# Inverting the 64x64 triangular systems of an RWKV-7 layer: substitution on VectorE cut to 16x16 blocks, the rest as small products on TensorE

## The chip, the core and the metric

The kernel runs on one core of one Trainium2 chip. The metric is the device time of one execution in microseconds (us), as the median of several runs. PE is TensorE (with PEld its weight loads), DVE is VectorE, ACT is ScalarE, POOL is GpSimd, SP is SyncE; L971 is line 971 of the kernel.

## The reference, cut to what matters

The model has two layers over 512 positions of 1024 channels, all in 32-bit floats. Layer 0 mixes positions by a spatial gate, layer 1 by RWKV-7, and a gated feed-forward block with a short convolution follows each. Only RWKV-7 is touched. Its heart is a recurrence over 512 positions in each of 16 heads of 64 channels:

```python
def step(state, inp):
    r_t, w_t, k_t, v_t, a_t, b_t = inp
    sa = jnp.einsum('bhvk,bhk->bhv', state, a_t)
    state = (state * w_t[:, :, None, :]
             + sa[..., None] * b_t[:, :, None, :]
             + v_t[..., None] * k_t[:, :, None, :])
    y_t = jnp.einsum('bhvk,bhk->bhv', state, r_t)
    return state, y_t
```

Taken in chunks of 64 positions, the recurrence inside a chunk is a triangular system: with L the strictly triangular 64x64 matrix of the products of a and b in the chunk, the inverse of (1 - L) gives all of the chunk's `sa` at once. There are 16 heads times 8 chunks, so 128 such systems.

## The kernel before

The program runs the phases one after another: gate layer, feed-forward, RWKV-7, feed-forward, final norm. Inside RWKV-7 four pieces matter.

**Pairs** (`pairs`, `decay`, `operands`, `products`): for each of 8 pairs of heads, the operands of the recurrence are made, mostly on DVE and ACT, and multiplied on PE (L893, L908). The masked products (L897 on DVE) hold the systems; ACT copies them into `ti[g]` (L898), where g is 0 for the pairs 0 to 3 and 1 for the pairs 4 to 7. So `ti[0]` and `ti[1]` each hold 64 systems, two to a column of blocks (one in the upper 64 partitions, one in the lower).

**Inversion** (`invert(g)`): each system is cut into 32x32 blocks. The 128 diagonal blocks of one g lie in one tile, 32 of them for each quarter of the partitions, and DVE's 32x32 transposes (L962) turn them so that a block fills the elements of one partition. Then the inverse of all 128 blocks is made at once by forward substitution: for each column j of 0 to 30, DVE multiplies (L970) and adds (L971) over 128 partitions and (31-j)(j+1) elements. Two transposes bring the inverses back (L976 into `z`, L977 into `y`, its transposed form), ACT copies `y` into the diagonal blocks of `ti` (L981), and two rounds of 32x32 products on PE, 64 in each (L991, L994), with copies by ACT between and behind (L999, L1001), make the off-diagonal block of each 64x64 inverse.

**Scan** (`scan(g)`): 8 chunks in order for each g. A chunk is a chain: PE products with the state (L1066, L1070), copy to `wt` by DVE (L1068), PE product with the inverse in `ti[g]` (L1079), copies to `vu` by DVE and ACT (L1080, L1081), PE products for the next state (L1086) and the output (L1091), and the sum into the next chunk's `vu` on DVE (L1089). In the chunk 1 the gate's weights are loaded by DMA and rounded by ACT and DVE (`gate_weights`). `finish` normalises two chunks at a time.

**Filling work**: the large 128x512 products of the key and value projections (`projections`, recorded at L284 to L286), the two small products of each value column (`value`, L790 and L804), and later the output projection (`project`).

The order is written by `weave`: a main generator is stepped, and after each of its steps a fill generator advances by `rate` and a side generator by `side_rate`, both in steps marked by `yield`. `RATES` holds these numbers. During the pairs 4 to 6 and then 7 the side generator is `invert(0)`; during `scan(0)` it is `invert(1)`. Each engine runs its queue in order. `invert` has one yield after the transposes, one for each two columns of the substitution, one behind the transposes back, and one for each half of a round of products.

Of the kernel before, what the change touches and what calls it, by code (L numbers as in the profile page):

```python
# [11 lines left out]
F32 = mybir.dt.float32  # L12
F32R = mybir.dt.float32r
AF = mybir.ActivationFunctionType
ALU = mybir.AluOpType
# [4 lines left out]
P = 128  # L20
# [30 lines left out]
NG = 2 * 16 + 8  # L51


COFF = dict(ident=0, bones=128, center=256, masks=384, smask=512, causal=1024, blk2=1152, one=1154, id2=1155)
NCST = 1219


def constants():
    c = np.zeros((P, NCST), np.float32)
    i = np.arange(P)  # L60
    same = (i[:, None] // C) == (i[None, :] // C)
    c[:, 0:128] = np.eye(P)
    c[:, 128:256] = same
    c[:, 256:384] = np.eye(P) - same / C
    s, t = (i % C)[:, None], np.arange(C)[None, :]
    c[:, 384:448] = s < t
    c[:, 448:512] = s <= t
# [4 lines left out]
    c[:, 1155:1219] = (i % C)[:, None] == np.arange(C)[None, :]  # L72
    return c


# [68 lines left out]
class Emit:  # L144
# [558 lines left out]
    def rwkv_main(self, r, ctx, gain):  # L703
        nc, tc, A = self.nc, self.tc, self.A
        V, S, G = nc.vector, nc.scalar, nc.gpsimd
# [5 lines left out]
        ip = r.ip  # L711
# [230 lines left out]
        def invert(g):  # L942

            tg = ti[g].rearrange("p i c t -> p (i c) t")
            Q = [(slice(64 * hd + 32 * b, 64 * hd + 32 * b + 32), slice(32 * b, 32 * b + 32))
                 for hd in range(2) for b in range(2)]

            def blocks(tag):  # L950
                return ip.tile([P, 32, 32], F32, tag=tag, bufs=1, name=self.uid(tag))

            x, li, tt = blocks("ix"), blocks("li"), blocks("tt")
            pr = ip.tile([P, 272], F32, tag="pr", bufs=1, name=self.uid("pr"))
            G.memset(tt, 0.0)
            G.memset(tt.rearrange("p s t -> p (s t)")[:, 0:1024:33], 1.0)
            for n, (rows, cols) in enumerate(Q):
                if g == 1 and n % 2 == 0:
                    V.tensor_copy(x[rows], tg[rows, :, cols])
                else:  # L960
                    S.copy(x[rows], tg[rows, :, cols])
            V.transpose(li.rearrange("p s t -> p t s"), x.rearrange("p u t -> p t u"))  # L962
            for _ in range(WAIT):
                yield
            for j in range(31):
                ni, nj = 31 - j, j + 1
                a = li[:, j, j + 1:32].unsqueeze(1).to_broadcast([P, nj, ni])
                b = tt[:, 0:nj, j].unsqueeze(2).to_broadcast([P, nj, ni])
                q = pr[:, 0:ni * nj].rearrange("p (c i) -> p c i", i=ni)
                V.tensor_tensor(q, a, b, ALU.mult)  # L970
                V.tensor_tensor(tt[:, 0:nj, j + 1:32], tt[:, 0:nj, j + 1:32], q, ALU.add)  # L971
                if j % 2 == 1:
                    yield

            z, y = blocks("ix"), blocks("li")
            V.transpose(z.rearrange("p u t -> p t u"), tt)  # L976
            V.transpose(y.rearrange("p u t -> p t u"), tt.rearrange("p s t -> p t s"))  # L977
            yield
            off = blocks("tt")
            for rows, cols in Q:  # L980
                S.copy(tg[rows, :, cols], y[rows])  # L981
            for i in range(2):
                for hf in range(2):
                    ps = self.acc("aux").rearrange("p (u t) -> p u t", t=32)
                    us = slice(16 * hf, 16 * hf + 16)
                    for u in range(16):
                        for hd in range(2):
                            b0, b1 = Q[2 * hd][0], Q[2 * hd + 1][0]
                            n = 16 * hf + u
                            if i == 0:  # L990
                                nc.tensor.matmul(ps[b1, u, :], tg[b0, n, 32:64], z[b0, n, :], start=True, stop=True,  # L991
                                                 tile_position=(b0.start, b1.start))
                            else:
                                nc.tensor.matmul(ps[b0, u, :], off[b1, n, :], y[b1, n, :], start=True, stop=True,  # L994
                                                 tile_position=(b1.start, b0.start))
                    for hd in range(2):
                        b0, b1 = Q[2 * hd][0], Q[2 * hd + 1][0]
                        if i == 0:
                            S.copy(off[b1, us], ps[b1])  # L999
# [283 lines left out]
```

## Time and profile before

| what | value |
|---|---|
| median of 3 runs (lowest, highest) | 1319.26 us (1318.08, 1319.82) |
| the profiled execution | 1317.32 us |
| its span, first to last instruction | 1315.5 us |
| PE, PEld, DVE, ACT, POOL busy, share of the span | 97%, 78%, 64%, 47%, 11% |
| mean granted TensorE clock | 0.978 |
| PE share of the chain that ended last | 78% |
| DVE share of that chain | 9% |

A PE that counts as busy need not be at its peak: matmuls overlap, and the end of each is modelled. The weight loads (PEld) have ends of their own, so their busy share tells better how tightly PE's work is packed. A group row reads: line, engine, operation, output and inputs, shapes, count, then busy time in us and mean ns of one, then idle time of the engine before it and what ended it. A 32-bit product leaves two records on PE, so the 128 products of L991 in the program (64 for each g) are 256 records. A row of windows has, behind the stretch and its length, the busy us of PE, PEld, DVE, ACT and POOL with the number of instructions, the granted TensorE clock, the share of the DMA engines and GB/s. A row of the chain of waits is a start, a length, and who held the chain.

### The profile page before, as it was taken

Reading aid. Unit: us, or ns where it says so; the run is one execution under the profiler, and the core shown is the slowest. Engines: PE = TensorE matmul, PEld = TensorE weight load, DVE = VectorE, ACT = ScalarE, POOL = GpSimd, SP = SyncE. Lnnn points to the kernel's source line nnn. Section 1 sums busy time; section 2 is a strip of 40 time slices with the busy share of each in tenths; the row PEclk is TensorE's granted clock in tenths of the full one; section 3 lists DMA queues with packets and bytes.
Section 4 is the critical chain, followed back from the end, with each engine's and each line's share of the span. In section 5 each row is a group of like instructions: output and inputs, shape, how many; then the busy total and the mean of one; then the engine's idle time right before and its main releaser. Section 6 shows DMA issues by size and latency. Waiting matters only on the chain.

```text
span 1315.5 us, 19526 instructions
## 1 busy us (share of the span) xinstructions
PE 1272.7 (97%) x7618; PEld 1031.3 (78%) x7618; DVE 848.5 (64%) x1365; ACT 623.8 (47%) x1062; POOL 142.8 (11%) x152
## 2 busy tenths in 40 slices
PE   8999999999999999999999998898999999999996
PEld 6878888888888888787777766676888888888886
DVE  5565488788874444865869785656687777772223
ACT  5444455555554333565657644333554444442221
POOL 3100200000000010310111012332300000000001
PEclk9999999999999999999979996999999999999998
DMA  7332345555556753245877786881333232333322
GB/s 259 88 113 80 106 151 170 167 168 174 166 173 211 224 150 108 79 136 157 251 220 205 225 209 147 207 221 41 96 96 97 96 96 96 97 92 91 101 89 76
DMA packets 100461, 188.55 MB, mean 143 GB/s; under 512 B 16912, under 2 KB 47760, under 8 KB 100368
## 3 DMA queue, kind: packets, MB, share of 16 engines
q10 hardware_dynamic: 36448, 109.46, 27.2%
q1 hardware_dynamic: 63920, 77.84, 20.7%
q8 instruction: 60, 0.98, 0.3%
q14 instruction: 33, 0.27, 0.1%
HBM read 146.70 MB, written 40.57 MB: 142 GB/s over the span
## 4 chain that ended last, share of the span: by engine, by line
PE 78%; DVE 9%; ACT 3%; issue 2%; DMA 2%; POOL 1%; ACTq 0%; DVEq 0%; SPq 0%; POOLq 0%
PE mm L284 8%; PE mm L285 8%; PE mm L286 8%; PE e L284 5%; PE e L286 5%; PE e L285 5%; PE us L284 5%; PE us L286 5%; PE us L285 5%; PE aux L284 5%; PE aux L286 5%; PE aux L285 5%; DVE tt L971 1%; DVE pr L970 1%; PE us L1066 1%
## 5 line engine op out<-in xcount | busy, mean ns | idle before, releaser
L212 ACT CAST wh<-w 128x512 fp32r<-128x512 f32 (+1 forms) x361 | 220.1, 612 | 398.8 <-PE mm L285 97.1
L213 DVE TENSOR_TENSOR wl<-w,wh 128x512 fp32r<-128x512 f32 x353 | 243.8, 692 | 186.9 <-ACT wh L212 182.8
L284 PE MATMUL mm<-mxh,wh 128*128 128x512 f32 x392 | 161.2, 412 | 0.6 <-DVE h L1166 0.4
L285 PE MATMUL mm<-mxl,wh 128*128 128x512 f32 x392 | 155.7, 397 | 0.6 <-DVE mxl L1139 0.6
L286 PE MATMUL mm<-mxh,wl 128*128 128x512 f32 x392 | 155.9, 398 | 0.3 <-DVE wl L213 0.3
L311 POOL TENSOR_TENSOR ss<-ss,sq 128x512 f32<-128x512 f32 x30 | 40.7, 1357 | 777.3 <-issue 594.8
L284 PEld LDWEIGHTS mm<-mxh,wh 128*128 128x128 f32 x392 | 74.8, 191 | 20.1 <-issue 3.2
L507 ACT ACTIVATE cv<-z,par 128x512 f32<-128x512 f32 x88 | 71.7, 817 | 36.0 <-DVE z L505 35.9
L286 PEld LDWEIGHTS mm<-mxh,wl 128*128 128x128 f32 x392 | 74.7, 191 | 17.3 <-DVE wl L213 0.6
L285 PEld LDWEIGHTS mm<-mxl,wh 128*128 128x128 f32 x392 | 74.8, 191 | 16.3 <-DVE mxl L1139 1.3
L284 PE MATMUL e<-mxh,wh 128*128 128x512 f32 x216 | 84.5, 391 | 0.0
L284 PE MATMUL us<-mxh,wh 128*128 128x512 f32 (+1 forms) x216 | 84.4, 391 | 0.0
L286 PE MATMUL us<-mxh,wl 128*128 128x512 f32 (+1 forms) x216 | 84.1, 389 | 0.0
L285 PE MATMUL us<-mxl,wh 128*128 128x512 f32 (+1 forms) x216 | 84.1, 389 | 0.0
L285 PE MATMUL e<-mxl,wh 128*128 128x512 f32 x216 | 84.0, 389 | 0.0
L286 PE MATMUL e<-mxh,wl 128*128 128x512 f32 x216 | 84.0, 389 | 0.0
L508 DVE SCALAR_TENSOR_TENSOR cv<-z,par,cv 128x512 f32<-128x512 f32 x88 | 66.1, 752 | 23.9 <-ACT cv L507 23.9
L284 PE MATMUL aux<-mxh,wh 128*128 128x512 f32 x208 | 81.2, 391 | 0.2 <-ACT wh L212 0.2
L286 PE MATMUL aux<-mxh,wl 128*128 128x512 f32 x208 | 81.1, 390 | 0.0
L285 PE MATMUL aux<-mxl,wh 128*128 128x512 f32 x208 | 80.9, 389 | 0.0
L509 DVE SCALAR_TENSOR_TENSOR cv<-z,par,cv 128x512 f32<-128x512 f32 x88 | 66.0, 752 | 2.9
L284 PEld LDWEIGHTS e<-mxh,wh 128*128 128x128 f32 x216 | 40.6, 188 | 8.7 <-issue 0.5
(1071 smaller groups left out, 2679.4 us busy)
## 6 DMA issues: line engine op xcount, KB each, us to landing
w<-in_wup ACTq DMA_DIRECT2D x88, 512.0 KB, 3.5
w<-in_wdn ACTq DMA_DIRECT2D x32, 512.0 KB, 3.6
st<-std SPq DMA_DIRECT2D x32, 384.0 KB, 5.8
std<-lq SPq DMA_DIRECT2D x32, 256.0 KB, 4.6
w<-in_wdn ACTq DMA_DIRECT2D x16, 384.0 KB, 3.3
w<-in_wsu ACTq DMA_DIRECT2D x8, 512.0 KB, 3.5
w<-in_wso ACTq DMA_DIRECT2D x8, 512.0 KB, 3.5
pw<-in_wk SPq DMA_DIRECT2D x16, 256.0 KB, 3.9
```

The source lines that it names most:

```text
L212: nc.scalar.copy(hi[r, :n], src)
L213: (lo_eng or nc.vector).tensor_tensor(lo[r, :n], src, hi[r, :n].bitcast(F32), ALU.subtract)
L284: mm(acc, wh, xh, start=first, stop=False)
L285: mm(acc, wh, xl, start=False, stop=False)
L286: mm(acc, wl, xh, start=False, stop=last)
L311: nc.gpsimd.tensor_tensor(self.ss, self.ss, self.sq, ALU.add)
L507: nc.scalar.activation(c, z[:, 2:], AF.Identity, scale=cw(2, i), bias=self.p("conv_b", l * 44 + i))
L508: nc.vector.scalar_tensor_tensor(c, z[:, 1:T + 1], cw(1, i), c, ALU.mult, ALU.add)
L509: nc.vector.scalar_tensor_tensor(c, z[:, 0:T], cw(0, i), c, ALU.mult, ALU.add)
L970: V.tensor_tensor(q, a, b, ALU.mult)
L971: V.tensor_tensor(tt[:, 0:nj, j + 1:32], tt[:, 0:nj, j + 1:32], q, ALU.add)
L1066: nc.tensor.matmul(us[H[hd], 0, i, :], ar(i, hd, 0), vu[:, hd, i, :], start=True, stop=True)
```

## The change

The substitution stops at 16x16 blocks. Each partition now inverts the two 16x16 diagonal blocks of its 32x32 block in one instruction (an access pattern whose second dimension steps from the one to the other), for the columns 0 to 14 instead of 0 to 30. The rest of each 32x32 inverse is put together by three stages of products, each with a 32x32 stationary operand and 16 moving columns, in the PSUM tag `aux`:

- stage one: 128 products for each g (32 in each quarter of the partitions) of the block in `ti` with `z`; before it, POOL sets the first 16 columns of the diagonal blocks in `ti` to zero (after the copies have read them). DVE adds an identity (new constant `id4`) while it moves the result to `w`.
- stage two: 64 products (only the first 32x32 block of each system) of `y` with `w`; ACT copies the result into `z`.
- stage three: 128 products of `w` with `y`; ACT copies the result into `y`.

Behind them the copies and the two rounds of 32x32 products stand as before. ACT also fills one half of `w` with the identity. `w` uses the buffer `tt`, which the two transposes back have to have read. The side rates are changed with the number of yields (21 before, 16 now).

```diff
-RATES = ((1.9, 2), (1.9, 6, 2.2), (0.8, 2, 2), (0.7, 2), (2, 2), (0.7, 6, 2.2))
+RATES = ((1.9, 2), (1.9, 6, 1.7), (0.8, 2, 1), (0.7, 2), (2, 2), (0.7, 6, 2))
...
+            for rows, cols in Q:
+                G.memset(tg[rows, :, cols.start:cols.start + 16], 0.0)
+            def diag(t, s0, t0, *ap):
+                return bass.AP(tensor=t.tensor, offset=32 * s0 + t0, ap=[[1024, P], [16 * 32 + 16, 2], *ap])
...
-            for j in range(31):
-                ni, nj = 31 - j, j + 1
...
+            for j in range(15):
+                ni, nj = 15 - j, j + 1
+                a = diag(li, j, j + 1, [0, nj], [1, ni])
+                b = diag(tt, 0, j, [32, nj], [0, ni])
+                o = diag(tt, 0, j + 1, [32, nj], [1, ni])
+                q = pr[:, 0:2 * ni * nj].rearrange("p (d c i) -> p d c i", d=2, i=ni)
                 V.tensor_tensor(q, a, b, ALU.mult)
-                V.tensor_tensor(tt[:, 0:nj, j + 1:32], tt[:, 0:nj, j + 1:32], q, ALU.add)
+                V.tensor_tensor(o, o, q, ALU.add)
...
+            def small(out, lhs, rhs, rows):
+                for n in range(32):
+                    for r0 in rows:
+                        nc.tensor.matmul(out[r0, n, :], lhs(r0, n), rhs(r0, n), start=True, stop=True,
+                                         tile_position=(r0.start, r0.start))
+            id4 = self.c("id4", 32).unsqueeze(1)
+            w = blocks("tt")
+            S.copy(w[:, :, 16:32], id4[:, :, 16:32].to_broadcast([P, 32, 16]))
...
+            q = bank()
+            small(q, lambda r0, n: tg[r0, n, col[r0.start]], lambda r0, n: z[r0, n, 0:16], quads)
+            V.tensor_tensor(w[:, :, 0:16], q, id4[:, :, 0:16].to_broadcast([P, 32, 16]), ALU.add)
+            yield
+            q = bank()
+            small(q, lambda r0, n: y[r0, n, :], lambda r0, n: w[r0, n, 0:16], firsts)
+            for r0 in firsts:
+                S.copy(z[r0, :, 0:16], q[r0])
+            yield
+            q = bank()
+            small(q, lambda r0, n: w[r0, n, :], lambda r0, n: y[r0, n, 16:32], quads)
+            S.copy(y[:, :, 16:32], q)
+            yield
```

New line numbers: L980 and L981 are the substitution (L970 and L971 before), L986 and L987 the transposes back, L993 all three stages, L1008 the sum into `w`, L1021 to L1041 the old copies and products (L981 to L1001), and from there on 40 more than before (L1066 is L1106).

**Where the instructions stand.** First place: PE's queue in `scan(0)`, from the chunk 2 to the chunk 4. `us_` and `e_` are the PSUM tiles of the scan's chunk products, `aux_` those of the inversion. Before, the chunk 2's last products are followed by both halves of the first round for g = 1:

```order
L1086 MATMUL us_7114<-vu_6976,cbt_6975 64x64 x8
L1091 MATMUL e_7115<-vu_6976,st_6974 64x64 x8
L991 MATMUL aux_7218<-ix_7175,ti_5021 32x32 x32
L991 MATMUL aux_7253<-ix_7175,ti_5021 32x32 x32
L1066 MATMUL us_7302<-vu_7107,st_7105 64x64
L1070 MATMUL e_7303<-vu_7107,st_7105 64x64
...
L1079 MATMUL us_7302<-wt_7312,ti_5020 64x64 x8
L1091 MATMUL e_7303<-vu_7107,st_7105 64x64
L1117 MATMUL aux_7325<-cst,y_6881 128x128 x4
L994 MATMUL aux_7334<-li_7176,tt_7213 32x32 x32
L994 MATMUL aux_7369<-li_7176,tt_7213 32x32 x32
L1086 MATMUL us_7302<-vu_7107,cbt_7106 64x64 x8
```

Now the three stages (L993) stand there, one piece between each two steps of the chunks 2 and 3, and the old rounds are spread over the chunks 3 and 4:

```order
L993 MATMUL aux_7488<-ix_7448,ti_5021 32x16 x128
L1106 MATMUL us_7632<-vu_7388,st_7386 64x64
...
L1157 MATMUL aux_7655<-cst,y_7186 128x128 x4
L993 MATMUL aux_7664<-tt_7486,li_7449 32x16 x64
L1119 MATMUL us_7632<-wt_7642,ti_5020 64x64 x8
L993 MATMUL aux_7741<-li_7449,tt_7486 32x16 x128
L1126 MATMUL us_7632<-vu_7388,cbt_7387 64x64 x8
L1131 MATMUL e_7633<-vu_7388,st_7386 64x64 x8
L1031 MATMUL aux_7896<-ix_7448,ti_5021 32x32 x32
L1106 MATMUL us_7940<-vu_7626,st_7624 64x64 x8
L1110 MATMUL e_7941<-vu_7626,st_7624 64x64 x8
L1031 MATMUL aux_7965<-ix_7448,ti_5021 32x32 x32
```

What moved: the first product of the inversion still stands behind the chunk 2's last one, but the inversion now ends in the chunk 4 instead of the chunk 3.

Second place: DVE's queue at the start of `scan(0)`. `rt` is the sum of a value column, `wt` and `vu` are the chunk 0's copies, `pr`, `tt`, `ix` and `li` belong to the inversion of g = 1. Before, the substitution is spread between the copies of the chunks 0 to 2:

```order
L806 TENSOR_TENSOR rt_4363<-mm_6863,v_6827 128x512
L970 TENSOR_TENSOR pr_6784<-li_6782,tt_6783 128x247
L971 TENSOR_TENSOR tt_6783<-tt_6783,pr_6784 128x13x19
L970 TENSOR_TENSOR pr_6784<-li_6782,tt_6783 128x252
L1068 COPY wt_6892<-us_6882 128x256
L971 TENSOR_TENSOR tt_6783<-tt_6783,pr_6784 128x14x18
L970 TENSOR_TENSOR pr_6784<-li_6782,tt_6783 128x255
L971 TENSOR_TENSOR tt_6783<-tt_6783,pr_6784 128x15x17
L1080 COPY vu_6773<-us_6882 64x256
```

Now all of it, and both transposes back, stand ahead of the chunk 0's first copy:

```order
L980 TENSOR_TENSOR pr_7085<-li_7083,tt_7084 128x30
L981 TENSOR_TENSOR tt_7084<-tt_7084,pr_7085 128x2x15
L807 TENSOR_TENSOR rt_4363<-mm_7168,v_7132 128x512
L986 STREAM_TRANSPOSE ix_7448<-tt_7084 128x32x32
L987 STREAM_TRANSPOSE li_7449<-tt_7084 128x32x32
L1108 COPY wt_7197<-us_7187 128x256
L1120 COPY vu_7074<-us_7187 64x256
```

What moved: the transposes back, which stood behind the chunk 2's copies, now stand directly ahead of the chunk 0's.

Third place: PE's queue in the pair 6 and 7, for g = 0. `mm_` tiles are the filling work, `us_` and `aux_` those of L893 (L894 now). Before, the first round of 32x32 products stands inside the pair 7's first products:

```order
L893 MATMUL us_6571<-ar_6353,bk_6358 128x128 x3
L991 MATMUL aux_6503<-ix_6494,ti_5020 32x32 x32
L893 MATMUL aux_6570<-ar_6353,bk_6358 128x128 x4
L893 MATMUL us_6571<-ar_6353,bk_6358 128x128
L804 MATMUL mm_6659<-rt_4362,wb_6657 128x512
L991 MATMUL aux_6587<-ix_6494,ti_5020 32x32 x32
```

Now the stages stand in the pair 6, with filling work between them:

```order
L993 MATMUL aux_6381<-ix_6323,ti_5020 32x16 x128
L285 MATMUL mm_6580<-mxh_5679,wh_6255 128x512
L286 MATMUL mm_6580<-mxl_5680,wh_6255 128x512
L287 MATMUL mm_6580<-mxh_5679,wl_6256 128x512
L285 MATMUL mm_6580<-mxh_5686,wh_6255 128x512
L993 MATMUL aux_6511<-tt_6379,li_6324 32x16 x64
```

What moved: the inversion's PE work starts about half a pair earlier than before, and its first round of 32x32 products now stands between the pairs 6 and 7.

More of the change, by code (lines that the diff above doesn't have):

```diff
@@ L51 @@
 NG = 2 * 16 + 8
-COFF = dict(ident=0, bones=128, center=256, masks=384, smask=512, causal=1024, blk2=1152, one=1154, id2=1155)
-NCST = 1219
+COFF = dict(ident=0, bones=128, center=256, masks=384, smask=512, causal=1024, blk2=1152, one=1154, id2=1155, id4=1219)
+NCST = 1251
 def constants():
@@ L72, in constants @@
     c[:, 1155:1219] = (i % C)[:, None] == np.arange(C)[None, :]
+    c[:, 1219:1251] = (i % 32)[:, None] == np.arange(32)[None, :]
     return c
@@ L953, in invert @@
             x, li, tt = blocks("ix"), blocks("li"), blocks("tt")
[L954 removed]
+            pr = ip.tile([P, 128], F32, tag="pr", bufs=1, name=self.uid("pr"))
             G.memset(tt, 0.0)
@@ L977, in invert, with bank @@
             V.transpose(y.rearrange("p u t -> p t u"), tt.rearrange("p s t -> p t s"))
+            yield
[7 more added lines that the diff above has]
+            S.copy(w[:, :, 16:32], id4[:, :, 16:32].to_broadcast([P, 32, 16]))
+            def bank():
+                return self.acc("aux").rearrange("p (u t) -> p u t", t=16)
+            col = {q[0].start: q[1] for q in Q}
+            quads, firsts = [q[0] for q in Q], [q[0] for q in Q[::2]]
+            q = bank()
[10 more added lines that the diff above has]
+            S.copy(y[:, :, 16:32], q)
             yield
```

3 lines of the change are left out of this document (removed).

## The prediction

> **What bounds the kernel now.** I read the page first (PE is busy for 97% of the span and carries 78% of the chain), then cut the part that the change touches into stretches: the pairs with the first inversion (700 to 757 us), the filling work before the scan (757 to 772), and `scan(0)` with the second inversion (772 to 839). Columns: PE, PEld, DVE, ACT, POOL busy, clock, DMA share, GB/s. The stretch 640 to 656 holds pairs without an inversion, 480 to 490 nothing but large products.
>
> ```profile
> 480.00:490.00 10.00, 10.00 (x45) 8.04 (x44) 3.33 (x5) 3.01 (x5) 0.00 (x0) 1.00 0.33 92
> ...
> 640.00:656.00 16.00, 15.80 (x139) 12.52 (x138) 13.72 (x21) 11.65 (x22) 2.69 (x3) 1.00 0.90 273
> ...
> 700.00:757.00 57.00, 54.14 (x621) 42.05 (x621) 47.78 (x105) 38.16 (x77) 5.93 (x4) 0.97 0.75 213
> 757.00:772.00 15.00, 14.34 (x78) 10.91 (x76) 11.43 (x26) 8.72 (x17) 2.92 (x6) 1.00 0.86 200
> ...
> 791.00:805.00 14.00, 9.11 (x221) 7.61 (x222) 11.61 (x25) 5.78 (x12) 3.33 (x4) 0.81 0.57 128
> 805.00:822.00 17.00, 15.83 (x292) 14.05 (x292) 5.21 (x14) 8.97 (x16) 2.63 (x3) 0.50 0.63 149
> ```
>
> Two engines are near their limit in the pairs: DVE with 47.78 of 57 us, and PE, whose weight loads fill 42.05 of 57 us (74%), against 78% without an inversion and 80% in pure large products. From 791 on it is different: a chain waits. The chain of waits shows both:
>
> ```profile
> 713.46 0.85 DVE tt L971
> 714.31 0.60 DVE lq L897
> ...
> 720.70 0.60 DVE dg L886
> ...
> 741.39 1.92 DVE ix L976
> 743.35 1.20 PE aux L991 x64
> ...
> 776.64 5.57 DMA w<-in_g
> ...
> 799.34 1.91 DVE ix L976
> 801.29 3.62 PE aux L991 x128
> ```
>
> In the pairs it runs over DVE's substitution and the pairs' own DVE work; in the scan it runs over the end of the substitution, a transpose and the first round of products. What these cost the scan is seen in where its chunks start (first row of the chunks 2 to 7, and of the next scan):
>
> ```profile
> 791.15 0.34 PE L1066 MATMUL us<-vu,st 128*64 128x64 f32 x4
> 804.85 0.49 PE L1066 MATMUL us<-vu,st 128*64 128x64 f32 x4
> 815.93 0.53 PE L1066 MATMUL us<-vu,st 128*64 128x64 f32 x4
> 822.13 0.53 PE L1066 MATMUL us<-vu,st 128*64 128x64 f32 x4
> 829.64 0.33 PE L1066 MATMUL us<-vu,st 128*64 128x64 f32 x2 [1.22 <-DVE vu L1089]
> 834.27 0.33 PE L1066 MATMUL us<-vu,st 128*64 128x64 f32 x2
> 839.19 0.34 PE L1066 MATMUL us<-vu,st 128*64 128x64 f32 x4
> ```
>
> The chunk 7 alone takes 839.19 - 834.27 = 4.9 us. The chunks 2 and 3, with the inversion's end among them, take 13.7 and 11.1.
>
> **The change part by part.** *DVE gives back.* The substitution's two lines, with three of their sizes:
>
> ```profile
> L970 DVE TENSOR_TENSOR pr<-li,tt 128x31 f32<-128x31 f32 (+15 forms) x62 | 22.2, 359 | 1.4
> L971 DVE TENSOR_TENSOR tt<-tt,pr 128x31 f32<-128x31 f32 (+15 forms) x62 | 23.0, 370 | 1.4
> ...
> L970 DVE TENSOR_TENSOR pr<-li,tt 128x60 f32<-128x60 f32 x4 | 0.8, 212 | 0.1
> L970 DVE TENSOR_TENSOR pr<-li,tt 128x135 f32<-128x135 f32 x4 | 1.2, 298 | 0.1
> L970 DVE TENSOR_TENSOR pr<-li,tt 128x256 f32<-128x256 f32 x2 | 0.8, 412 | 0.0
> ...
> L897 DVE TENSOR_TENSOR lq<-aux,cst 128x512 f32<-128x512 f32 x16 | 10.9, 682 | 9.7 <-PE aux L893 8.5 <-issue 1.1
> ```
>
> The 124 instructions took 45.2 us, 22.6 for each g. The 30 new ones of a g have 30 to 128 elements, 1360/15 = 91 on average; between the rows of 60 and 135 that is 212 + 86 x 31/75 = 248 ns, so 7.4 us. The sum into `w` reads 512 elements from PSUM, as L897 does: 0.7 us. DVE saves about 14.5 us for each g.
>
> *PE takes on.* 320 products for each g, 640 records (two each). The nearest rows are these, with the products of a whole array, of half rows and half columns, and of a quarter of each:
>
> ```profile
> 759.28 1.05 PE L790 MATMUL mm<-cst,v 128*128 128x128 f32 x8
> ...
> 795.93 0.68 PE L1091 MATMUL e<-vu,st 64*64 64x64 f32 x16
> ...
> 743.35 1.20 PE L991 MATMUL aux<-ix,ti 32*32 32x32 f32 x64 [1.66 <-DVE ix L976]
> 801.29 3.62 PE L991 MATMUL aux<-ix,ti 32*32 32x32 f32 x128 [4.68 <-DVE ix L976]
> ```
>
> 131, 42 and 19 ns a record. The two quarters of L991 run side by side, so the price follows the stationary columns over the tiles in use, about 1 ns for each column (128/1, 64/2, 32/2, plus a tail). The 16 moving columns should save nothing against 32. Stage two has two tiles: 128 x 19 ns = 2.4 us. Stages one and three use four tiles. If all four run side by side, each costs 256 x 9.5 = 2.4 us, so 7 us for each g; if no more than two do, 4.8 each, so 12 us. I take 7, since nothing in L991 shows two tiles in each other's way. At the clock of 0.50, by the row at 801.29 (28 ns), it is 11 to 18 us.
>
> A rule speaks against this. The Trainium skill, TensorE: Matmul & The Clock Gate, Part 1 (Wait — 56ns, not 53.3ns?), has a floor of about 25 ns from one matmul's start to the next, however small. By it 640 records would be an estimated 16 us for each g, and the change a clear loss. The 64 records in 1.20 us above, 19 ns each, lie below that floor, so the trace does not bear it out.
>
> *ACT and POOL.* ACT gains four copies for each g (two of 32x512 at 578 ns as L999, two of 128x512 at about 590 as L911), 2.3 us:
>
> ```profile
> L999 ACT COPY tt<-aux 32x512 f32<-32x512 f32 x8 | 4.6, 578 | 0.1
> ...
> 759.08 0.59 ACT L911 COPY bt<-us 128x512 f32<-128x512 f32 x1
> ```
>
> ACT has 19 us free in the pairs. POOL gains four memsets of 512 elements for each g, by the row below (1024 elements) at most 2.9 us; they wait for the copies of L961 and hold up the next POOL work behind them. POOL's 5.93 of 57 us hides that; without that cover the chunk 0's L1075 would be late by it.
>
> ```profile
> 756.05 1.43 POOL L955 MEMSET tt<- 128x1024 f32 x1 [27.68 <-PE aux L994]
> ```
>
> *Pairs, 700 to 757.* If DVE alone set the pace, 14.5 us would go. But PE's queue is the same plus 7 us. How tightly it can be packed, and what the clock took, these rows tell:
>
> ```profile
> 745.00:748.00 3.00, 3.00 (x10) 1.36 (x9) 1.44 (x3) 2.79 (x3) 0.00 (x0) 0.50 0.15 38
> ...
> 820.10:823.40 3.30, 3.30 (x53) 3.06 (x55) 2.26 (x5) 0.74 (x2) 2.72 (x3) 0.50 0.76 174
> ```
>
> Of the 42.05 us of loads, L991 and L994 have 256 records at 19 ns, 4.8 us; the other 37.3 us need 47.8 us at 78%, 40.1 at the 93% that narrow products reach (row at 820.10). With 4.8 + 7 that is 59.6 or 51.9, against 57 now. Most of the loads belong to large products (80%), so I take 84%: 44.4 + 11.8 = 56.2. The wait of 1.66 us ahead of L991 and the clock of 0.50 behind it are then gone. I forecast 1 us saved, between 6 saved and 5 lost (two tiles at a time, at 78% or a little better).
>
> *Start of the scan.* 757 to 772 is filling work that PE does at its own pace, and stays. But both transposes back (1.9 us each) now stand ahead of the chunk 0's `wt` copy, and ACT's fill of `w` waits for them with the chunk's `vu` copy and the gate's DMA queued behind. The chunks 0 to 2 start up to 3.8 us later; part of the transposes falls before the chunk's products end, so I take 1.3. The DMA of 5.57 us at 776.64 then holds the chunk 1 as before, so the DVE time freed there is worth nothing.
>
> *Chunks 2 to 5.* Two prices that are still missing:
>
> ```profile
> 769.90 1.10 PE L804 MATMUL mm<-rt,wb 128*128 128x512 f32 x2 [0.29 <-issue]
> ...
> L981 ACT COPY ti<-li 32x1024 f32<-32x1024 f32 x8 | 8.3, 1042 | 8.2 <-DMA wl<-wvd 4.2 <-DVE li L977 4.0
> ```
>
> The wait of 4.68 us before L991 goes, since the substitution ends before the chunk 0. Chunk 2: 4.9, the last L790 and L804 (1.05 + 1.10), stage one (2.4): 9.4 instead of 13.7. Chunk 3: 4.9 + 4.8 for the stages two and three + 1.2 for half of the first round, less 1.0 that falls into the chain's own gaps: 9.9 instead of 11.1. Chunk 4: 4.9 + 1.2 + 2.4 is 8.5, instead of 6.2; ACT's eight copies ahead of the `vu` copy (4 x 1.04 + 4 x 0.58 = 6.5) just fit. Chunk 5: about 7, from 7.5. Together 34.8 instead of 829.64 - 791.15 = 38.5. With the 1.3, the scan saves 2.5 to 3.
>
> Sum: 1 + 3 = 4 us from the profiled 1317.3, so 1313.3. That execution lies 1.9 under the median, which gives **1315.3 us** against 1319.26.
>
> **The rivals.** *Slower: the clock stays low in the chunks 3 to 5.* The granted clock fell to 0.50 with the idle time at 797, and these rows show what held it there:
>
> ```profile
> 809.80:813.20 3.40, 3.40 (x124) 3.24 (x124) 1.12 (x4) 1.39 (x3) 0.00 (x0) 0.50 0.41 97
> ...
> 823.00:839.00 16.00, 12.87 (x237) 10.79 (x235) 10.82 (x28) 4.62 (x12) 5.51 (x8) 0.99 0.89 201
> ```
>
> 3.4 us packed with nothing but L994's 32x32 products did not bring the clock back; the 3.3 us at 820.10, packed with 64-wide chunk products, did (0.99 behind it). So small products may count as idling, and the change adds 7 us of them where little else runs. Then the stages cost 11 instead of 7, the old rounds 7 instead of 4, the chunk products 2 more: 9 lost against the 4 saved above: +5, so 1324. It decides if more than one of the windows between the chunks 2 and 5 is granted 0.50. For it: the rows. Against it: the wait that dropped the clock is gone. The Trainium skill, TensorE: Matmul & The Clock Gate, Part 1, has the clock halved by an idle window of about 3.4 us and restored by a busy one; by that rule no drop would come, and the row at 809.80 differs from it.
>
> *Faster: DVE did set the pace in the pairs*, as the chain says. PE then packs better than 0.80, and the pairs give 6 and the scan 5: 1308. Against it: the 0.74 that PE has already.
>
> *No difference*: the stages cost on PE what DVE gives back, to within 2.6 us. For it: the count of the pairs above.
>
> **How the numbers follow.** About 0.2% (2.6 us) can be told from no change. The forecast's own case (2.6 to 8 us saved) has 0.38, the faster rival 0.14, no difference 0.23, slower 0.25: faster 0.52, same 0.23, slower 0.25. The range takes in the forecast, no difference, and most of both rivals: 1307 to 1324.
>
> **What would show it.** L980 and L981 together near 15 us; stage one near 2.4 us, not 4.8; no wait of PE over 1 us before the stage in the chunk 2; chunks 2 to 5 together near 35 us; the stretch from the first L962 transpose to the second inversion's copies unchanged within 5 us. The prediction is wrong if that stretch shrinks by 10, or if the clock reads 0.50 through the chunks 3 to 5.

## The result, and the profile after

The changed kernel takes 1352.12 us, the median of four runs (1350.52 to 1354.62); the kernel before took 1318.67 on the same chip. The ratio is 1.0258, with a 95% interval of 1.0235 to 1.0281: 33 us slower, where 4 us faster was forecast. The profiled execution has a span of 1348.7 us, against 1315.5. One execution of the run filler (2135 us) and one of cutonly (6496 us) fell far from all others and are left out of their medians below.

From the page of after, the busy time and the two queues that carry instructions:

```profile
PE 1294.1 (96%) x8898; PEld 1050.3 (78%) x8898; DVE 824.4 (61%) x1303; ACT 628.7 (47%) x1070; POOL 144.9 (11%) x160
...
q8 instruction: 70, 1.15, 0.3%
q14 instruction: 33, 0.27, 0.1%
```

and the row of q8 from the page of before:

```profile
q8 instruction: 60, 0.98, 0.3%
```

q8 brings PE's instructions, 16 KB in a packet. Ten packets more is what the change adds: 640 products, of two loads (PEld) and two passes (PE) each, are 2560 instructions, 256 to a packet. Neither the count of instructions nor this row was used in the prediction.

The groups by line of after, for the substitution and for the three stages (busy, mean ns | idle time before them and what ended it):

```profile
L980 DVE TENSOR_TENSOR pr<-li,tt 128x30 f32<-128x30 f32 (+7 forms) x30 | 7.9, 265 | 0.9
L993 PE MATMUL aux<-tt,li 32*32 32x16 f32 x256 | 7.7, 210 | 4.1 <-issue 4.1
L981 DVE TENSOR_TENSOR tt<-tt,pr 128x30 f32<-128x30 f32 (+7 forms) x30 | 7.5, 251 | 0.7
...
L993 PE MATMUL aux<-li,tt 32*32 32x16 f32 x512 | 6.6, 195 | 6.6 <-issue 6.6
...
L993 PE MATMUL aux<-ix,ti 32*32 32x16 f32 x512 | 5.2, 182 | 5.2 <-issue 5.2
```

DVE's part came out as forecast: 7.9 + 7.5 = 15.4 us for both g. The products have something new: idle time of 4.1 + 6.6 + 5.2 = 15.9 us that ended with "issue", so with no wait that the profile shows; one more hole, of 1.6 us, stands inside the chunk products behind them (L1126). Together they are 17.4 us. PE's timeline tells where it lies. The stages of the first inversion (start, length, and in brackets the idle time before):

```profile
726.63 2.01 PE L993 MATMUL aux<-ix,ti 32*32 32x16 f32 x218
731.84 0.73 PE L993 MATMUL aux<-ix,ti 32*32 32x16 f32 x38 [3.20 <-issue]
...
734.50 2.52 PE L993 MATMUL aux<-tt,li 32*32 32x16 f32 x86
738.56 1.35 PE L993 MATMUL aux<-tt,li 32*32 32x16 f32 x42 [1.54 <-issue]
...
746.23 1.69 PE L993 MATMUL aux<-li,tt 32*32 32x16 f32 x181
750.83 0.81 PE L993 MATMUL aux<-li,tt 32*32 32x16 f32 x75 [2.90 <-issue]
```

and of the second one, in the scan:

```profile
815.14 1.73 PE L993 MATMUL aux<-ix,ti 32*32 32x16 f32 x185
818.82 0.78 PE L993 MATMUL aux<-ix,ti 32*32 32x16 f32 x71 [1.96 <-issue]
...
825.62 3.07 PE L993 MATMUL aux<-tt,li 32*32 32x16 f32 x108 [2.55 <-issue]
...
831.81 1.90 PE L993 MATMUL aux<-li,tt 32*32 32x16 f32 x128 [1.86 <-issue]
835.54 1.89 PE L993 MATMUL aux<-li,tt 32*32 32x16 f32 x124 [1.82 <-issue]
```

No stage runs through. A run of products stops in the middle, with no operand that it would wait for, and goes on 1.5 to 3.2 us later. The piece between two holes at 831.81 has 128 passes and as many loads: exactly one packet. The packets' own records fit: one starts at 729.49 and takes 0.94 us, and PE goes on at 731.84; so it goes on 1.4 us behind the packet's end. The next two holes end 1.3 us behind a packet's end.

Where this leaves the chunks, from the first rows of the chunks 2 to 6 of after:

```profile
809.44 0.34 PE L1106 MATMUL us<-vu,st 128*64 128x64 f32 x4
819.58 0.30 PE L1106 MATMUL us<-vu,st 128*64 128x64 f32 x2
843.16 0.69 PE L1106 MATMUL us<-vu,st 128*64 128x64 f32 x8
854.81 0.69 PE L1106 MATMUL us<-vu,st 128*64 128x64 f32 x8
862.94 0.33 PE L1106 MATMUL us<-vu,st 128*64 128x64 f32 x2 [1.22 <-DVE vu L1129]
```

The chunks 2 to 5 take 862.94 - 809.44 = 53.5 us, against 38.5 before and 34.8 forecast; the chunk 3, with the stages two and three, takes 23.6. Two stretches of after, with the columns of the prediction's windows (the clock is the third from the end), add the clock:

```profile
820.00:840.00 20.00, 12.18 (x445) 11.03 (x442) 2.46 (x7) 3.15 (x5) 0.00 (x0) 0.50 0.50 115
840.00:855.00 15.00, 14.41 (x364) 13.27 (x362) 4.14 (x9) 9.13 (x16) 4.44 (x5) 0.50 0.40 94
```

In the first of them PE is idle for 7.8 of 20 us. The clock is 0.50 from 820.0 to 857.6, so also through the second, where PE is busy for 14.41 of 15 us.

The loss has two places of like size. From the first L970 (L980) to the scan's first product the time grows from 772.3 - 702.5 = 69.8 to 790.1 - 702.5 = 87.6 us, 17.8 more; `scan(0)` grows from 66.9 to 82.8, 15.9 more. The rest is as before.

### The profile page after: what moved, and what is told of

It is laid out like the page before. It is cut to its first block, busy times and chain, and to the rows that moved or that the text cites. A ratio compares the mean times of both kernels' runs of the same rounds, so it can differ in the third digit from the quotient of the medians.

```text
span 1348.7 us, 22052 instructions
## 1 busy us (share of the span) xinstructions
PE 1294.1 (96%) x8898; PEld 1050.3 (78%) x8898; DVE 824.4 (61%) x1303; ACT 628.7 (47%) x1070; POOL 144.9 (11%) x160
## 4 chain that ended last, share of the span: by engine, by line
PE 83%; DVE 4%; issue 3%; ACT 3%; DMA 2%; POOL 1%; ACTq 0%; DVEq 0%; SPq 0%; POOLq 0%
PE mm L285 8%; PE mm L286 8%; PE mm L287 8%; PE e L285 5%; PE e L287 5%; PE e L286 5%; PE us L285 5%; PE us L287 5%; PE us L286 5%; PE aux L285 5%; PE aux L287 5%; PE aux L286 5%; PE aux L993 1%; DMA w<-in_wo 1%; PE aux L909 1%
## 5 line engine op out<-in xcount | busy, mean ns | idle before, releaser
L287 PEld LDWEIGHTS mm<-mxh,wl 128*128 128x128 f32 x392 | 75.1, 192 | 17.6 <-DMA wl<-wkd 0.8
L509 DVE SCALAR_TENSOR_TENSOR cv<-z,par,cv 128x512 f32<-128x512 f32 x88 | 66.1, 752 | 23.9 <-ACT cv L508 23.9
```

What stands on the lines that cost most here:

```text
L287: mm(acc, wl, xh, start=False, stop=last)
L509: nc.vector.scalar_tensor_tensor(c, z[:, 1:T + 1], cw(1, i), c, ALU.mult, ALU.add)
```

## The experiments

Theory A, supply: PE takes short instructions faster than they can be brought, a packet of 256 in a fixed time, and the holes are PE waiting for the next packet. Theory B, clock: small products count as idling, the clock halves, and that costs the time. Theory C, price: a product on a 32x32 tile is far dearer than forecast.

**The products alone, behind the kernel's end ("tail").** On the kernel before:

```diff
+        def run(tiles, cols):
+            q = e.acc("aux")
+            for n in range(384):
+                r0 = 32 * (n % tiles)
+                r, o = slice(r0, r0 + 32), cols * (n % (T // cols))
+                mm(q[r, o:o + cols], ident[r, r], wide[r, o:o + cols], start=True, stop=True,
+                   tile_position=(r0, r0))
...
+        run(4, 16)
...
+        run(1, 16)
...
+        run(1, 128)
```

Expected: 

> The kernel before with a tail of TensorE work that nothing reads, behind the last phase: three runs of 384 products (1536 instructions, 6 packets of 256) with 32x32 stationary blocks: 16 moving columns on four tiles, 16 columns on one tile, 128 columns on one tile; eight products of 128x128 by 512 columns ahead of each and behind. Supply theory: the first two runs both take about 4 x 3.9 + 4 = 20 us in bursts of 256 records (loads and passes together) with a hole behind each, whatever the number of tiles; the third is slower than its packets (768 x 50 to 60 ns, about 42 us) and has no hole. Price theory: the run on four tiles has the holes, the run on one tile has none and takes 768 x 25 ns, 19 us, evenly. Clock theory: both run evenly, at 0.50 once the first 4 us have passed.

PE's timeline of the run on four tiles:

```profile
1310.92 2.06 PE L1283 MATMUL aux<-cst 32*32 32x16 f32 x220
1315.76 1.90 PE L1283 MATMUL aux<-cst 32*32 32x16 f32 x128 [2.77 <-issue]
1319.49 1.90 PE L1283 MATMUL aux<-cst 32*32 32x16 f32 x128 [1.83 <-issue]
1322.97 1.90 PE L1283 MATMUL aux<-cst 32*32 32x16 f32 x128 [1.58 <-issue]
1326.46 1.90 PE L1283 MATMUL aux<-cst 32*32 32x16 f32 x128 [1.58 <-issue]
1330.20 0.72 PE L1283 MATMUL aux<-cst 32*32 32x16 f32 x36 [1.84 <-issue]
```

and of the run on one tile with 16 columns:

```profile
1339.95 37.55 PE L1283 MATMUL aux<-cst 32*32 32x16 f32 x768
```

Nothing here waits for another engine, and from 1313.5 on the DMA is nearly idle. On four tiles, 128 passes and their loads go through in 1.90 us, then comes a hole; from one burst's start to the next it takes 3.5 to 3.7 us. The records of the five packets start at 1313.36, 1316.91, 1320.60, 1324.05 and 1327.60, the last four about 1.1 us behind the start of a burst, and PE goes on 2.4 to 2.6 us after a packet's start. That fits a next packet that is asked for only when the one before it is begun. So PE gets 256 instructions in about 3.6 us, 14 ns for each. On one tile an instruction takes 37.55 us / 1536 = 24 ns, and there is no hole at all. That is theory A with its number. The expectation of holes on one tile was wrong, since these products are slower than the supply; against C speaks that the dearer products, not the cheaper, run evenly. The third run, with 128 columns, was expected to take 42 us and took 158.5, so 206 ns a pass, nearly all of it at the clock of 0.50; the price of such products was forecast far too low.

The Trainium skill, Runtime: NRT & Kernel Launch, section Instruction fetch mechanics, has the instructions arrive in blocks of 16 KiB, 256 of them, the next one brought while the current one is executed; the runs agree. It calls that cost mostly hidden, since instructions are sent out slower than a block is filled. Here that does not hold: 1.90 us of work stand against 3.6 us of supply.

**What a pass costs ("prices").** Again a tail, of short runs that lie within the packets that are there:

```diff
+        for what in ((48, 32, 4, 16), (48, 32, 2, 16), (48, 32, 1, 16), (24, 64, 2, 64), (24, 64, 1, 64),
+                     (96, 32, 4, 256), (24, 32, 2, 256), (24, 64, 1, 256)):
+            large()
+            run(*what)
```

Expected: 

> The kernel before with a tail that nothing reads: short runs, each behind six products of 128x128 by 512 columns so that its packets are there: 48 products (192 instructions) of 32x32 by 16 columns on four tiles, on two, on one; 24 of 64x64 by 64 columns on two tiles and on one; then 96 of 32x32 by 256 columns on four tiles, 24 on two tiles, 24 of 64x64 by 256 columns on one. Supply theory: no hole in any run; a record (load or pass) costs about 5 to 6 ns on four tiles, 11 on two and 24 or less on one at full clock. Price theory: four tiles cost no less than two. Clock theory: the long run on four tiles counts as busy and keeps the full clock, that on two 32x32 tiles falls to 0.50; if even four tiles of 32x32 fall to 0.50, the products of the stages can hold the clock down by themselves.

PE's timeline: four, two and one tile with 16 columns, and the long run on four tiles.

```profile
1308.07 0.99 PE L1283 MATMUL aux<-cst 32*32 32x16 f32 x96
...
1314.34 1.69 PE L1283 MATMUL aux<-cst 32*32 32x16 f32 x96
...
1321.32 3.21 PE L1283 MATMUL aux<-cst 32*32 32x16 f32 x96
...
1344.98 10.56 PE L1283 MATMUL aux<-cst 32*32 32x256 f32 x192
```

No hole anywhere, at full clock. A pass with its load takes 10.3, 17.6 and 33.4 ns on four, two and one tile (10 to 12, 22 and up to 48 were expected). For a g that is 512 x 10.3 + 128 x 17.6 = 7.5 us: the forecast of 7 was right for the array's time, and C falls. The floor of about 25 ns from matmul to matmul (the Trainium skill, TensorE: Matmul & The Clock Gate, Part 1, Wait — 56ns, not 53.3ns?) is undercut on two and on four tiles. But in the supplied pace of the tail, 128 passes in 3.6 us, a pass takes 28 ns: for the long runs of this kernel, a count by that floor (an estimated 16 us a g) would have come near the truth, for another reason.

As for B: the 10.56 us on four tiles, with 256 columns, kept the full clock, whereas the one-tile run of the tail went on at 0.50, busy throughout:

```profile
1350.00:1370.00 20.00, 20.00 (x379) 20.00 (x378) 0.00 (x0) 0.00 (x0) 0.00 (x0) 0.50 0.01 2
```

So products on one small tile, without a hole, did not hold the full clock, and those on four tiles did. A long run of 16 columns on four tiles without holes was not made. The run on two 32x32 tiles, for which 0.50 was expected, kept 1.00, but lasted only 5.37 us.

**A quarter of the instructions ("quarter").**

```diff
-                for n in range(32):
+                for n in range(0, 32, 4):
...
-                        nc.tensor.matmul(out[r0, n, :], lhs(r0, n), rhs(r0, n), start=True, stop=True,
+                        nc.tensor.matmul(out[r0, n:n + 4, :], lhs(r0, n), rhs(r0, slice(n, n + 4)),
```

Expected: 

> Leaves out three of four products of every stage: each remaining one multiplies four systems' columns by the first system's block, so the values are wrong, while the same 512 columns move and every output column is written. 80 products a g instead of 320, so 320 instructions of TensorE (two loads and two passes each) instead of 1280. Supply theory (TensorE's instructions arrive in packets of 256, about 3.9 us apart when it outruns them): about 7 or 8 of the 10 added packets go (62 or 63 on the queue q8), the idle 'issue' time inside the products goes, and the time falls to 1312 to 1322. Clock theory (small products count as idling, the low clock costs the time): at most 10 of the 33 us come back, 1342 or more. Price theory (a product on a 32x32 tile costs far more than 9.5 ns a record): the time falls also, but what is left of the products still shows holes in proportion to their number.

Measured: 1328.91 us, ratio 1.0078 (1.0050 to 1.0107), 62 packets. Two thirds of the loss are gone with three quarters of the instructions, the 512 columns being the same, though the time lies 7 us over the expected range. Its stages run without such a hole, but holes come up behind them, in the old products and the scan's (PE's timeline):

```profile
810.13 0.75 PE L1031 MATMUL aux<-ix,ti 32*32 32x32 f32 x35
813.93 0.63 PE L1031 MATMUL aux<-ix,ti 32*32 32x32 f32 x29 [3.06 <-issue]
816.02 1.92 PE L1031 MATMUL aux<-ix,ti 32*32 32x32 f32 x64
...
821.86 1.11 PE L1119 MATMUL us<-wt,ti 64*64 64x64 f32 x14 [3.51 <-issue]
```

The two holes are about 256 instructions apart (127 passes and as many loads). The scan's own products are short too; the supply is used up by whatever stands in a row.

**Twice the products ("double").**

```diff
+                        for _ in range(2):
+                            nc.tensor.matmul(out[r0, n, :], lhs(r0, n), rhs(r0, n), start=True, stop=True,
+                                             tile_position=(r0.start, r0.start))
```

Expected: 

> Every product of the stages issued twice in a row, same result: 640 products and 2560 instructions a g, 80 packets. Supply theory: the ten further packets take 3.6 us each with next to nothing of it hidden, since the first ten have used up what lay ready: 36 us more, 1383 to 1395. Price theory without packets (8 us a g more at full clock, 16 at half): 1368 to 1380.

Measured: 1386.01 us, ratio 1.0508 (1.0482 to 1.0533), 80 packets. The first ten packets cost 33.4 us, the next ten 1386.0 - 1352.1 = 33.9: 3.4 us for each, both times, and in the pairs 17 us for five. The bound of C without packets (1380) is passed. The 3.4 us are the price of 256 such instructions here, not of a hole: the holes grew from 17.4 to 32.0 us, by 14.6 of the 33.9.

**Each half alone ("cutonly", "addonly").** The first leaves out the stages:

```diff
-            def small(out, lhs, rhs, rows):
...
-            small(q, lambda r0, n: w[r0, n, :], lambda r0, n: y[r0, n, 16:32], quads)
-            S.copy(y[:, :, 16:32], q)
-            yield
+            for _ in range(3):
+                yield
```

Expected: 

> The cut of the substitution alone: the three stages of products, the fill of w and their copies are left out, so the off-diagonal 16x16 parts are missing and the values are wrong; the three yields stay. It shows what the time given back by DVE (14.5 us a g) is worth. If PE sets the pace of the pairs, only its wait of 1.66 us and the 3.4 us at half clock go there, and in the scan the wait of 4.68 us with part of the low clock: 1308 to 1315. If DVE set the pace (the faster rival of the prediction), the pairs alone give 10 or more: 1296 to 1304.

The second adds products to the kernel before, and nothing else but the side rates for three more steps:

```diff
             yield
+            for lhs, rhs, rows in ((None, z, quads), (y, z, firsts), (z, y, quads)):
+                out = self.acc("aux").rearrange("p (u t) -> p u t", t=16)
+                for n in range(32):
+                    for r0 in rows:
+                        l = tg[r0, n, col[r0.start]] if lhs is None else lhs[r0, n, :]
+                        nc.tensor.matmul(out[r0, n, :], l, rhs[r0, n, 0:16], start=True, stop=True,
+                                         tile_position=(r0.start, r0.start))
+                yield
```

Expected: 

> The products alone: the substitution stays as before, and the same 320 products a g go into banks that nothing reads, between the transposes back and the first round (rates 2.5, 2.3, 2.5 for three more steps). Supply theory: 70 packets as in the changed kernel, the same holes, and nearly the whole loss: 1345 to 1360. If the loss comes from the new chain of copies and sums between the stages, or from POOL's memsets, most of it is gone: 1320 to 1330.

Measured: cutonly 1316.82 us, ratio 0.9992 (0.9980 to 1.0003), just over the expected 1308 to 1315; addonly 1351.84 us, ratio 1.0272 (1.0249 to 1.0296), 70 packets. The products alone give the whole loss, so nothing of it need be put down to copies, sums and memsets. And the time given back by DVE is worth, in this order of the work, at most 2.6 us by the interval. Another execution of the same kernel ("cutonly2"), of 1319.59 us, shows why:

Expected: 

> The cut of the substitution alone once more, for its trace (its first profiled execution took five times as long as all others and can't be read). 62 of TensorE's packets or fewer, no hole of 256 records. If PE sets the pace of the pairs, the scan starts within 4 us of 772 although DVE is busy some 14 us less there; what is gained at the first round of the scan (the wait of 4.68 us) is lost again at a later wait of the scan.

The stretch from the first L970 (L980) to the scan, in before and in cutonly2 (the fourth number is DVE's busy time):

```profile
702.50:772.30 69.80, 66.91 (x686) 51.65 (x685) 57.35 (x130) 44.45 (x87) 8.85 (x9) 0.98 0.79 215
```

```profile
700.50:770.90 70.40, 65.81 (x686) 51.14 (x685) 46.19 (x106) 44.41 (x87) 8.51 (x13) 0.98 0.79 213
```

and two rows of cutonly2's waits between 790 and 832 (waited for: us, times, longest; its L1079 is a chunk's first product, its L1007 the second round):

```profile
PE us L1079 <- DMA vu<-vtd: 4.0, 1, 4.0
...
PE aux L1007 <- issue: 2.0, 1, 2.0
```

In the pairs DVE is busy for 46.19 us instead of 57.35, and the stretch is no shorter: DVE did not set the pace there. Nor did PE pack tighter, being idle for 4.6 us instead of 2.9. In the scan the chunk 2 takes 6.4 us instead of 13.7, as the vanished wait promised. But the chunk 0 takes 12.9 instead of 9.4, behind the transposes back; the chunk 3 waits 4.0 us for the next one's loads at its end, and stays at 11.0 against 11.1; and the chunk 4, with old rounds in it, a hole of 2.0 and the clock at 0.50 from 804.9 to 825.4, takes 13.1 instead of 6.2. The clock falls ahead of that hole, and the old rounds run at it. The gain is given back within two chunks.

**Array time without instructions ("pework").** On the kernel before:

```diff
+            for _ in range(3):
+                out = self.acc("aux")
+                for _ in range(3):
+                    nc.tensor.matmul(out, self.c("ident", P), self.c("smask", T), start=True, stop=True)
+                yield
```

Expected: 

> The kernel before with array time but few instructions: at the place of each stage three products of 128x128 by 512 columns (0.9 us each at full clock, 12 instructions for the three) into a bank that nothing reads, 8.1 us and 36 instructions a g (rates 2.5, 2.3, 2.5). 60 packets. If the loss is the packets' alone, 1317 to 1322. If PE's time counts in full wherever it is put, 16 us more in all: 1331 to 1336. Between them it shows how much of the 34 us is plain work on a full engine.

Measured: 1323.02 us, ratio 1.0041 (1.0022 to 1.0061), 60 packets. 16 us of array time cost 5, just over the end of what the supply theory allowed. The stretch to the scan takes 72.9 us instead of 69.8 with 8.1 of array time in it; PE's idle time there fell from 2.9 to 1.0 us, and the 3.4 us at half clock are gone. In the scan a hole of 4.39 us ending with "issue" stands in the old second round (L999 there), at the packet count of before. So plain work of some 7 us a g costs little here, though not nothing.

**The same instructions, spread ("spread"), and array time in the holes ("filler").** Spread puts each stage into four pieces with a bank of their own, and steps of filling work between them:

```diff
+            for ns in PIECES:
+                q = bank()
+                small(ns, q, lambda r0, n: tg[r0, n, col[r0.start]], lambda r0, n: z[r0, n, 0:16], quads)
+                V.tensor_tensor(w[:, ns, 0:16], q[:, ns], id4[:, :, 0:16].to_broadcast([P, PIECE, 16]), ALU.add)
+                yield
...
-            while side_due >= 1:
+            while side_due >= 1 or due >= 1:
+                if side_due >= 1:
...
```

Expected: 

> The same 320 products a g and 1280 instructions, but in pieces of 8 systems (128 instructions, 64 in the second stage), each with its own bank and its own copy, put between steps of the pairs, of the scan and of the filling products; rates 2.4, 1.4, 2.4 for the more pieces. Supply theory: in the pairs the packets arrive during the large products, so that stretch loses next to nothing; in the scan few large products are left, and half of the loss there may stay: 1315 to 1332. Price theory: the same number of dear products, 1350 or more. Clock theory: no idle window of their own in the pairs, 1340 to 1345.

Measured: 1345.70 us, ratio 1.0211 (1.0184 to 1.0237), 70 packets: 5 to 6 us better than the change, 14 over the range expected by supply, and next to the 1340 to 1345 of the clock theory (the six runs lie between 1339 and 1353). In the pairs its "issue" holes fall to under 0.4 us each, as expected, and yet that stretch takes 83.2 us, 13.4 more than before. Its 9 us of products, by pework's price, and 10 us more at the clock of 0.50, by the price below, make an estimated 8 of it; the rest is open. So the holes cannot be the whole loss. In the scan five holes of 0.9 to 3.0 us stay, and `scan(0)` takes 86.3. Spreading needs long products to stand between, and the scan has few.

Filler adds a product of a whole array ahead of every four systems:

```diff
+                    if n % 4 == 0:
+                        nc.tensor.matmul(out[:, 4 * (n // 4):4 * (n // 4) + 4, :], self.c("ident", 128),
+                                         self.c("masks", 64), start=True, stop=True)
```

Expected: 

> Adds eight products of a whole array (128x128 by 64 columns) to each of the three stages, one ahead of every four systems; their output is overwritten by the products that follow, so the result is the changed kernel's. 24 products a g at about 4 x 66 ns are 6.3 us of array time a g, with 96 instructions. Supply theory: the array time falls into the holes, and only the 96 instructions (0.4 of a packet, 1.5 us a g) cost: 1352 to 1357. Price theory: the work stands beside the dear products: 12 to 13 us more, 1364. Clock theory: whole-array products bring the clock back, 1340 to 1348.

Measured: 1371.3 us, ratio 1.0409 (1.0384 to 1.0434), which no theory expected. The groups of filler:

```profile
L993 PE MATMUL aux<-cst 128*128 128x64 f32 x96 | 28.6, 394 | 0.0
...
L996 PE MATMUL aux<-tt,li 32*32 32x16 f32 x256 | 9.8, 212 | 0.0
L996 PE MATMUL aux<-li,tt 32*32 32x16 f32 x512 | 9.4, 203 | 1.2 <-issue 1.2
L996 PE MATMUL aux<-ix,ti 32*32 32x16 f32 x512 | 8.7, 192 | 2.1 <-issue 2.1
```

The holes shrank from 15.9 to 3.3 us, so array time does go into them. But the added products took 28.6 us, not 12.6, and the clock was at 0.50 for 79 us of the stretch and the scan, instead of 55. As a test of the cause it is inconclusive, and its forecast failed.

**The first inversion only ("first").** `invert(1)` is the old function; the rest is the change.

Expected: 

> The change in the first inversion only, the second as before. If each loss belongs to its own place, the 18 us of the pairs stay and the 16 us of the scan go: 1333 to 1341. If the scan suffers from what the pairs leave behind (later start, clock, packets out of step), over 1343.

Measured: 1335.29 us, ratio 1.0148 (1.0116 to 1.0179), within the expected range, 65 packets. `scan(0)` is back at 67.7 us (its traced execution took 1342.22): each inversion pays for itself, where it stands.

**Holes and half clock, side by side.** From the first L970 (or its successor) to the end of `scan(0)` in each trace: the sum of PE's holes of over 0.5 us that end with "issue", and the time at the clock of 0.50. The last column is the difference of the medians.

| run | packets on q8 | holes, us | at 0.50, us | slower than before, us |
|---|---|---|---|---|
| before | 60 | 0 | 27.3 | |
| after | 70 | 17.4 | 54.6 | 33.4 |
| addonly | 70 | 15.6 | 64.9 | 34.7 |
| double | 80 | 32.0 | 88.7 | 67.9 |
| first | 65 | 10.1 | 37.5 | 18.1 |
| quarter | 62 | 6.6 | 20.5 | 11.4 |
| spread | 70 | 9.2 | 54.6 | 28.2 |
| filler | 70 | 2.8 | 79.4 | 53.8 |
| pework | 60 | 4.4 | 6.8 | 4.9 |
| cutonly | 60 | 2.0 | 27.3 | -0.3 |

Where the products stand in long rows, the holes are about half of the loss. In after, addonly, double and first the time at half clock is longer as well, and quarter gets rid of most of both, so it cannot tell the two apart. What quarter, double and addonly show together is that the loss goes with the number of the products' instructions.

**The clock's share.** The kernels before, prices and tail run the same code from the first L970 to the scan, with 3.4, 6.8 and 10.2 us of it at 0.50 in their traces, in 69.8, 71.3 and 72.7 us: 2.9 us for 6.8, so 0.43 us for each us at half clock. The change has 17.1 us there, 13.7 more, or an estimated 6 of its 17.8. The holes of the first inversion add up to 3.20 + 1.54 + 2.90 = 7.6, and the 4 that are left may be array time (pework's 8.1 us cost 3.1). For `scan(0)` the three read 66.9, 66.4 and 66.5 with 23.9, 17.1 and 17.1 us: no slope to speak of. That does not carry over to after, where PE is idle for only 0.6 us in the chunk 4, at 0.50 throughout. What lowers the clock was not varied by itself. In after it falls at 731.3 and 820.0, within and behind the first holes, and in the tail at 1314.5, in the first hole. But in spread it falls at 762.3, and in cutonly2 at 804.9, where PE had waited for no packet, and for nothing longer than 0.7 and 0.9 us, in the 8 us before. So the holes are not its only cause, and how the loss divides between holes and clock is not settled.

## Why the prediction was wrong

- **The step that failed** is "PE takes on": "320 products for each g, 640 records (two each)", priced at 9.5 to 19 ns, "so 7 us for each g". The array's price was right (7.5 by the short runs). But the products are 1280 instructions in long rows, and in such rows they came at 13 ns each here and 14 in the tail. The stages took 5.9 + 5.4 + 5.4 = 16.8 us of the first inversion instead of 7, with 7.6 of holes in them and the rest partly at half clock. The row at 743.35, 64 passes in 1.20 us, could not show it: its 128 instructions are half a packet.
- **DVE gives back 14.5 us a g**: right in size (15.4 for L980 and L981 of both g). Worth: at most 2.6 us, by cutonly. In the pairs that was foreseen (the faster rival fell). In the scan, 3 us were forecast, from the wait of 4.68 that indeed went. What is late next, the loads of the chunk 4 and the old rounds that moved into it, was priced too low.
- **Pairs, 44.4 + 11.8 = 56.2**: the 11.8 was the wrong term by far, but the 44.4 was wrong too. It has PE pack tighter once DVE is relieved; without the stages that would be 44.4 + 4.8 = 49.2 instead of 57, so 8 us saved, and cutonly2 saved none. With stages of 7 us the pairs would by pework have lost an estimated 3 us, and not gained 1.
- **Start of the scan, +1.3**: the chunks 0 and 1 together took 19.3 us instead of 18.8, so 0.5. The number is near, by luck: the chunk 0 was 2.0 us longer and the chunk 1, forecast as unchanged, 1.4 shorter.
- **Chunks 2 to 5, 34.8**: the chunk 2 came as forecast (9.4; 10.1 with a hole of 1.96 in it). The chunk 3 took 23.6 instead of 9.9, with 7.8 of holes in it and nearly all of the rest at 0.50. The chunk 4 took 11.6 instead of 8.5 with no such hole: it ran at 0.50 from end to end, where its three half rounds took 1.92 us each instead of 1.2. In cutonly2, without the stages, it took 13.1, with one hole of 2.0. The scan's own sum, 38.5 - 34.8 - 1.3, is 2.4 us and not 2.5 to 3.
- **The slower rival** named the right sign and a clock that did stay at 0.50 through the chunks 3 and 4, at a price of 9 us. It took the clock for the cause. Its ground, that products on small tiles count as idling, was borne out for one tile, and not for four without holes. The low clock came together with the holes; they are 17.4 of the 33.4 us, and the clock's part is only estimated.

## What to carry to other kernels

Count instructions as well as array time: a fp32 product here is four, and in these runs rows of more than about 256 to 440 short instructions ran at the supply's pace, 256 in some 3.6 us, however small they were. Idle PE time that ends with "issue", together with more packets on q8, is the sign of it; a quarter of the products, with the same columns, took away two thirds of the loss, while putting long ones between removed holes and little of the time. And before work is moved off an engine, leave it out altogether for one run: cutting the substitution from 45.2 to 15.4 us of DVE gained at most 2.6 us here, so in this order of the work no way of doing it elsewhere could have paid more than that. No version here is clearly faster than the kernel before.

## What the runs showed of the hardware

- In the tail, PE went on 2.4 to 2.6 us after the start of a packet of 256 instructions, and 3.5 to 3.7 us passed from burst to burst with the DMA nearly idle. The first burst in the tail had 220 passes and their loads, so less than two packets lay ready.
- A pass of 16 columns with its load takes 10.3 ns when spread over four 32x32 tiles, 17.6 on two, 33.4 on one, at full clock.
- The tail's third run, 128 columns on one 32x32 tile and busy all the time, had a granted clock of 0.50 from 1393.0 us to beyond its end at 1545.6; 10.56 us of 256 columns on four tiles kept 1.00.
